# A broadcast row of per-token scales, made by two transfers through DRAM in place of a diagonal and a product with ones on TensorE

## The chip, the cores and the metric

The kernel runs on one core of a Trainium2 chip. The metric is the time of one execution on the device in microseconds (us), as the median of several runs. Beside it stands one profiled execution, whose trace gives the start and the length of every instruction on the engines: TensorE (PE, with its weight loads as PEld), VectorE (DVE), ScalarE (ACT), GpSimd (POOL) and SyncE (SP). DMAs are issued from the queues of SP and of POOL.

## The reference

Three residual blocks are applied to one sequence of 256 tokens with 2048 channels, all in float32: an attention layer that keeps the best keys by an index score, a block attention layer, and a third block of three-way sparse attention beside a gated linear recurrence, which ends in a gated feed-forward network (FFN). Each one begins with a root-mean-square norm:

```
def rms_norm(x, g):
    xf = x.astype(jnp.float32)
    y = xf * lax.rsqrt(jnp.mean(xf * xf, axis=-1, keepdims=True) + EPS)
    return (y * g.astype(jnp.float32)).astype(x.dtype)
...
    h2 = rms_norm_2(x, norm2_w[l])
    x = x + (jax.nn.silu(h2 @ w_ffn_gate[l]) * (h2 @ w_ffn_up[l])) @ w_ffn_down[l]
```

The norm's factor is one number for each token. The kernel multiplies by the gain before a product with the weights and by the token's factor after it, so that the product need not wait for the factor.

## The kernel before, in words

Tokens stand in two tiles of 128 partitions. The products with the weights stream about 394 MB, nearly all of it float32 weights, in tiles `raw` of mostly 1 MB from DRAM (queue of SP, three buffers). `weights` splits each half of a tile into a rounded part `wh` (ACT, line 135) and a rest `wl` (DVE, line 136), three buffers each, and PE multiplies both with the split activations. There are two kinds of product. `gemm` leaves tokens on the partitions; there the factor is a column of 128 numbers, one on each partition, which an engine takes as a scalar operand. `gemm_T` leaves channels on the partitions and tokens along the row; there the factor has to be a row of 256 numbers that stands on all 128 partitions. `row_of` makes that row from the two columns, and `joined` (lines 209 to 213) multiplies an evacuated product by it: two passes of `add_halves` (ACT line 206, DVE line 207) free the PSUM bank, then one DVE instruction multiplies by the row (line 213).

`row_of` is called five times: once in each of the two attention layers (`attn_layer`, line 595, the row is used from the gate products on), twice in `second` (line 1215), and once at the start of `ffn` (line 1373), where the first gate product is the next one to be evacuated. The columns come from `norm_rstd`: for each token tile a DVE sum (line 310) and four short POOL instructions (lines 298, 299, 313, 314).

Beside that work POOL issues small loads: the gains of the norms in set-up (`gains`, line 393), the constants of the third block (`gains2`, lines 405 to 408), the weights of its compression (`compress`, line 1036, read by the products `hid` in line 1044), the copy of x to DRAM (`park_x`, line 381), and the last gain in `ffn` (line 1376). Each engine works through its own list in order. The lists are laid out by the program's scheduler, which orders instructions by when it thinks they can run, with small side jobs deferred to steps of the large products; buffers come from rotating pools (`w2` has 28 buffers of 128x512). So an edit in one place can move instructions in another.

Of the kernel before, what the change touches and what calls it, by code (L numbers as in the profile page):

```python
# [11 lines left out]
F32 = mybir.dt.float32  # L12
F32R = mybir.dt.float32r
AF = mybir.ActivationFunctionType
ALU = mybir.AluOpType
AX = mybir.AxisListType

P = 128
T = 256
# [7 lines left out]
class Kern:  # L27
# [187 lines left out]
    def row_of(self, r):  # L215

        nc = self.nc
        b = self.bank("row")
        row = self.sb.tile([P, T], F32, tag="row", bufs=2, name="row")
        dg = self.w2("diag")[:, :T]  # L220
        for t in range(2):
            ts = slice(t * P, (t + 1) * P)
            nc.vector.tensor_scalar(dg[:, ts], self.ident, r[t], None, ALU.mult)
            nc.tensor.matmul(b[:, ts], self.ones, dg[:, ts], start=True, stop=True)
        nc.scalar.copy(row, b[:, :T])
        return row[:, None, :].to_broadcast([P, 2, T])

    def gemm_by_tile(self, xT, W, c0, n, evac, ng):
# [122 lines left out]
    def setup(self):  # L351
        nc, d, sb = self.nc, self.d, self.sb
        self.x = [[self.w2(f"x{t}{j}") for j in range(4)] for t in range(2)]
        self.load_x(0, d["x"][0])
        self.ident = sb.tile([P, P], F32, name="ident")
        nc.sync.dma_start(self.ident, d["c_ident"])
        zero = self.w2("zero")
        nc.vector.memset(zero, 0.0)
        warm = self.bank("warm")
        for _ in range(2):  # L360
            nc.tensor.matmul(warm, zero[:, :P], zero, start=True, stop=True)
        self.mhalf = sb.tile([P, 8], F32, name="mhalf")
        nc.vector.memset(self.mhalf, -0.5)
        self.ones = sb.tile([P, P], F32, name="ones")
        nc.vector.memset(self.ones, 1.0)
        self.gT = sb.tile([P, 64], F32, name="gT")
        g1 = self.w2("g1")[:, :P]
        nc.sync.dma_start(g1[:16, :], d["a_norm"].rearrange("a (k p) -> (a k) p", p=P))
        b = self.bank("gt")
        nc.tensor.transpose(b[:, 0:16], g1[:16, :], self.ident[:16, :16])  # L370
        nc.vector.tensor_copy(self.gT[:, 0:16], b[:, 0:16])
# [1194 lines left out]
```

## Time and profile before

| | |
|---|---|
| median of 3 runs | 2296.4 us (2295.2 to 2296.54) |
| the profiled execution's own time | 2295.19 us |
| its span in the trace | 2293.4 us, so 1.8 us lie around it |
| busy: PE, DVE, ACT, POOL | 99%, 65%, 50%, 6% of the span |
| mean granted clock of TensorE | 0.998 of full speed |
| weights and other data read from DRAM | 397.95 MB, 175 GB/s over the span |

The busy shares are means over the whole span. A line of the chain of waits or of the timeline says at which moment which engine was late; only there is an instruction worth its own length.

### The profile page before, as it was taken

To read this page: it belongs to the slowest core of one execution; us is meant where nothing else is said; L and a number is where in the kernel's file an instruction comes from. 1 tells how busy PE (TensorE), PEld (TensorE's weight loads), DVE (VectorE), ACT (ScalarE), POOL (GpSimd) and SP (SyncE) were. 2 spreads that over 40 slices of the span, in tenths; PEclk is the share of its full clock that TensorE was granted. 3 is DMA by queue.
4 is the path that set the end of the run, shared out by engine and by line. 5 is a ranking of instruction groups with operands and counts; after the bars stand their busy time and mean duration, and the time that the engine had idled before them with its cause. 6 is when DMAs were issued, how large, how long until landed. Compare 5 with 4: busy or idle time off the path is not lost.

```text
span 2293.4 us, 33719 instructions
## 1 busy us (share of the span) xinstructions
PE 2276.4 (99%) x13374; PEld 1939.6 (85%) x13374; DVE 1480.4 (65%) x2297; ACT 1146.2 (50%) x1966; POOL 136.0 (6%) x233
## 2 busy tenths in 40 slices
PE   9999999999999999999999999999999999999998
PEld 8878888888888888888888988888888888888887
DVE  5686775656775556789586666656665466655655
ACT  5555654556654434565563545545443344434444
POOL 1011100112100200000110000000000000000000
PEclk9999999999999999999999999999999999999999
DMA  7544455654456844454453576556555555555554
GB/s 228 189 159 147 129 184 183 190 184 147 152 184 202 250 141 149 132 161 151 134 173 111 177 227 192 185 183 202 184 184 190 194 185 184 186 195 188 184 186 145
DMA packets 308094, 404.33 MB, mean 176 GB/s; under 512 B 7376, under 2 KB 222384, under 8 KB 307936
## 3 DMA queue, kind: packets, MB, share of 16 engines
q1 hardware_dynamic: 305184, 394.04, 53.7%
q0 software_dynamic: 2752, 8.13, 1.2%
q8 instruction: 105, 1.72, 0.3%
q14 instruction: 53, 0.43, 0.1%
HBM read 397.95 MB, written 4.19 MB: 175 GB/s over the span
## 4 chain that ended last, share of the span: by engine, by line
PE 98%; DVE 1%; ACT 0%; DMA 0%; issue 0%; SPq 0%; POOL 0%; ACTq 0%; POOLq 0%
PE mm L189 31%; PE mm L191 16%; PE mm L163 14%; PE mm L164 14%; PE mm L165 14%; PE lg L490 1%; PE tr L344 1%; PE tp L269 1%; PE hid L1044 1%; PE pt L523 0%; PE ib L688 0%; PE nl L1136 0%; DMA x<-in_x_dram 0%; DVE wl L136 0%; PE ov L540 0%; PE cvb L791 0%
## 5 line engine op out<-in xcount | busy, mean ns | idle before, releaser
L136 DVE TENSOR_TENSOR wl<-raw,wh 128x1024 fp32r<-128x1024 f32 (+4 forms) x760 | 902.7, 1188 | 664.7 <-ACT wh L135 655.8
L135 ACT CAST wh<-raw 128x1024 fp32r<-128x1024 f32 (+4 forms) x760 | 776.5, 1022 | 838.9 <-PE mm L165 457.3
L189 PE MATMUL mm<-hl,wh 128*128 128x512 f32 x3072 | 1076.4, 395 | 2.0 <-DVE raw L207 1.2
L191 PE MATMUL mm<-hl,wl 128*128 128x256 f32 x3072 | 850.1, 284 | 0.1
L189 PEld LDWEIGHTS mm<-hl,wh 128*128 128x128 f32 x3072 | 568.9, 188 | 122.6 <-DVE raw L207 1.4
L191 PEld LDWEIGHTS mm<-hl,wl 128*128 128x128 f32 x3072 | 576.9, 188 | 12.6 <-DVE wl L136 0.4
L164 PE MATMUL mm<-wl,hl 128*128 128x512 f32 (+4 forms) x1504 | 574.4, 383 | 0.2 <-DVE wl L136 0.2
L165 PE MATMUL mm<-wh,hl 128*128 128x512 f32 (+4 forms) x1504 | 570.0, 381 | 0.0
L163 PE MATMUL mm<-wh,hl 128*128 128x512 f32 (+4 forms) x1504 | 529.6, 382 | 0.0
L164 PEld LDWEIGHTS mm<-wl,hl 128*128 128x128 f32 x1504 | 283.5, 189 | 55.2 <-issue 0.6
L165 PEld LDWEIGHTS mm<-wh,hl 128*128 128x128 f32 x1504 | 283.1, 188 | 55.1 <-issue 1.5
L163 PEld LDWEIGHTS mm<-wh,hl 128*128 128x128 f32 x1504 | 281.4, 189 | 56.5 <-issue 1.3
L298 POOL TENSOR_SCALAR rsqv<-nsum 128x1 f32<-128x1 f32 x10 | 3.5, 350 | 1188.1 <-DVE nsum L1418 733.2
L283 ACT ACTIVATE hl<-tp,gT 128x256 fp32r<-128x256 f32 x64 | 27.6, 471 | 22.1 <-PE tp L269 20.0
L284 DVE SCALAR_TENSOR_TENSOR hl<-tp,gT,hl 128x256 fp32r<-128x256 f32 x64 | 28.5, 478 | 12.7 <-ACT hl L283 12.5
L504 ACT ACTIVATE lg<-lg,nb 128x128 f32<-128x128 f32 (+1 forms) x64 | 28.4, 445 | 14.8 <-POOL nb L497 14.8
L206 ACT COPY up<-mm 128x256 f32<-128x256 f32 x44 | 16.4, 373 | 32.3 <-PE mm L191 32.3
L206 ACT COPY sg<-mm 128x256 f32<-128x256 f32 x44 | 16.4, 372 | 32.1 <-PE mm L191 32.1
L780 DVE SCALAR_TENSOR_TENSOR cv<-raw,cols,cv 128x255 f32<-128x255 f32 (+2 forms) x72 | 31.9, 475 | 0.2
L207 DVE TENSOR_TENSOR sg<-mm,sg 128x256 f32<-128x256 f32 x44 | 18.5, 421 | 15.5 <-ACT sg L206 15.5
L302 ACT ACTIVATE junk<-x 128x512 bf16<-128x512 f32 (+1 forms) x42 | 25.6, 610 | 5.5 <-DMA x<-in_x_dram 2.1
L207 DVE TENSOR_TENSOR up<-mm,up 128x256 f32<-128x256 f32 x44 | 18.5, 421 | 13.5 <-ACT up L206 13.5
(389 smaller groups left out, 1534.9 us busy)
## 6 DMA issues: line engine op xcount, KB each, us to landing
raw<-in_w_in_dram SPq DMA_DIRECT2D x76, 1024.0 KB, 5.2
raw<-in_w_ffn_gate_dram SPq DMA_DIRECT2D x44, 1024.0 KB, 5.1
raw<-in_w_ffn_up_dram SPq DMA_DIRECT2D x44, 1024.0 KB, 5.2
raw<-in_w_ffn_down_dram SPq DMA_DIRECT2D x41, 1024.0 KB, 5.0
raw<-in_a_w_in_dram SPq DMA_DIRECT2D x40, 1024.0 KB, 5.2
raw<-in_b_w_in_dram SPq DMA_DIRECT2D x40, 1024.0 KB, 5.1
raw<-in_a_w_out_dram SPq DMA_DIRECT2D x16, 1024.0 KB, 5.1
raw<-in_b_w_out_dram SPq DMA_DIRECT2D x16, 1024.0 KB, 5.2
```

Of the source, the lines that this page charges most:

```text
L135: nc.scalar.copy(wh, raw[:, k * h:k * h + k])
L136: nc.vector.tensor_tensor(wl, raw[:, k * h:k * h + k], wh.bitcast(F32), ALU.subtract)
L163: nc.tensor.matmul(o, xh, wh[:, c], start=first, stop=False)
L164: nc.tensor.matmul(o, xh, wl[:, c], start=False, stop=False)
L165: nc.tensor.matmul(o, xl, wh[:, c], start=False, stop=last)
L189: nc.tensor.matmul(self.c2(pt[m]), wh[:, c, ms], hl[:, c], start=first, stop=False)
L191: nc.tensor.matmul(pt[m][:, :T], wl[:, c, ms], hl[:, c, 0], start=False, stop=last)
L206: self.nc.scalar.copy(o, bank[:, T:])
L207: self.nc.vector.tensor_tensor(o, bank[:, :T], o, ALU.add)
L284: nc.vector.scalar_tensor_tensor(lo[:, k], tp[:, c], g, hi[:, k].bitcast(F32), ALU.mult, ALU.subtract)
L504: nc.scalar.activation(lgs[u][:, i * S:(i + 1) * S], lgs[u][:, i * S:(i + 1) * S], AF.Exp, bias=nbs[u][:, i:i + 1], accum_out=sms[t][:, h0 ...
L780: v.scalar_tensor_tensor(o[:, s:], x[:, :T - s], self.convw[:, k:k + 1], o[:, s:], ALU.mult, ALU.add)
```

## The change

The row is no longer computed on PE. Each of the two columns (128 partitions, one number each) is written to a DRAM tile `line` of 256 numbers by a DMA of POOL's queue, and a third DMA of the same queue reads the 256 numbers back onto all 128 partitions. The diagonal tiles on DVE, the products with ones on PE, the copy out of PSUM on ACT, the PSUM bank and the tile of ones go away.

```diff
     def row_of(self, r):
 
         nc = self.nc
-        b = self.bank("row")
+        line = self.dr.tile([T, 1], F32, tag="line", bufs=2, name="line")
         row = self.sb.tile([P, T], F32, tag="row", bufs=2, name="row")
-        dg = self.w2("diag")[:, :T]
         for t in range(2):
-            ts = slice(t * P, (t + 1) * P)
-            nc.vector.tensor_scalar(dg[:, ts], self.ident, r[t], None, ALU.mult)
-            nc.tensor.matmul(b[:, ts], self.ones, dg[:, ts], start=True, stop=True)
-        nc.scalar.copy(row, b[:, :T])
+            nc.gpsimd.dma_start(line[t * P:(t + 1) * P, :], r[t])
+        nc.gpsimd.dma_start(row, line.rearrange("t o -> o t").to_broadcast([P, T]))
         return row[:, None, :].to_broadcast([P, 2, T])
...
-        self.ones = sb.tile([P, P], F32, name="ones")
-        nc.vector.memset(self.ones, 1.0)
```

The scheduler lays the lists out anew. At the start of `ffn` POOL's list before has the chain of the first token tile, then the four loads of the last gain (`gf`), then the chain of the second tile:

```order
L298 TENSOR_SCALAR rsqv<-nsum 128x1 [waits DVE_49]
L299 TENSOR_TENSOR rstd_14704<-rsqv,mhalf 128x1 [waits Pool_49]
L313 TENSOR_SCALAR rstd_14706<-rstd_14704 128x1 [waits Pool_49]
L314 TENSOR_SCALAR rstd_14708<-rstd_14704 128x1
L1376 DMA gf_14732<-in_norm_f_w_dram 128x512 [waits DMASW5_49,PE_49]
L1376 DMA gf_14733<-in_norm_f_w_dram 128x512 [waits DMASW6_49,DMASW3_49,PE_49]
L1376 DMA gf_14734<-in_norm_f_w_dram 128x512 [waits DMASW7_49]
L1376 DMA gf_14735<-in_norm_f_w_dram 128x512
L298 TENSOR_SCALAR rsqv<-nsum 128x1 [waits DVE_49]
L299 TENSOR_TENSOR rstd_14705<-rsqv,mhalf 128x1 [waits Pool_49]
L313 TENSOR_SCALAR rstd_14707<-rstd_14705 128x1 [waits Pool_49]
L314 TENSOR_SCALAR rstd_14709<-rstd_14705 128x1
```

In the changed kernel (whose line numbers are 3 lower from line 226 of before on, and 5 lower from line 366 on) the same place of POOL's list reads as follows; line 221 writes a column to DRAM and line 222 reads the row back:

```order
L1371 DMA gf_14718<-in_norm_f_w_dram 128x512 [waits DMASW4_49]
L295 TENSOR_SCALAR rsqv<-nsum 128x1 [waits DVE_49]
L296 TENSOR_TENSOR rstd_14690<-rsqv,mhalf 128x1 [waits Pool_49]
L310 TENSOR_SCALAR rstd_14692<-rstd_14690 128x1 [waits Pool_49]
L311 TENSOR_SCALAR rstd_14694<-rstd_14690 128x1
L221 DMA line<-rstd_14690 128x1 [waits DMASW5_49]
L295 TENSOR_SCALAR rsqv<-nsum 128x1 [waits DVE_49]
L296 TENSOR_TENSOR rstd_14691<-rsqv,mhalf 128x1 [waits Pool_49]
L310 TENSOR_SCALAR rstd_14693<-rstd_14691 128x1 [waits Pool_49]
L311 TENSOR_SCALAR rstd_14695<-rstd_14691 128x1
L221 DMA line<-rstd_14691 128x1 [waits DMASW6_49]
L222 DMA row<-line 128x256 [waits DMASW7_49,DMASW6_49,DMASW5_49]
```

The four gain loads now stand ahead of both chains. The read of the row waits for both writes (DMASW5 and DMASW6 are their completion semaphores), and POOL has nothing to issue behind it before the end of the program.

DVE's list at the first gate evacuation of `ffn` before, where `sg` is the tile that takes the product and line 213 the multiplication by the row:

```order
L136 TENSOR_TENSOR wl<-raw,wh 128x1024 [waits DVE_49,DMAHW5_49,PE_49,Activation_49]
L207 TENSOR_TENSOR sg_14742<-mm,sg_14742 128x256 [waits Activation_49]
L136 TENSOR_TENSOR wl<-raw,wh 128x1024 [waits PE_49,Activation_49]
L207 TENSOR_TENSOR sg_14742<-mm,sg_14742 128x256 [waits Activation_49]
L136 TENSOR_TENSOR wl<-raw,wh 128x1024 [waits DMAHW6_49,PE_49,Activation_49]
L213 TENSOR_TENSOR sg_14742<-sg_14742,row 128x512 [waits DVE_49]
L136 TENSOR_TENSOR wl<-raw,wh 128x1024 [waits PE_49,Activation_49]
```

And in the changed kernel:

```order
L207 TENSOR_TENSOR sg_14725<-mm,sg_14725 128x256 [waits Activation_49]
L136 TENSOR_TENSOR wl<-raw,wh 128x1024 [waits DVE_49,DMAHW5_49,PE_49,Activation_49]
L207 TENSOR_TENSOR sg_14725<-mm,sg_14725 128x256 [waits Activation_49]
L213 TENSOR_TENSOR sg_14725<-sg_14725,row 128x512 [waits DMASW7_49,DVE_49]
L136 TENSOR_TENSOR wl<-raw,wh 128x1024 [waits PE_49,Activation_49]
L136 TENSOR_TENSOR wl<-raw,wh 128x1024 [waits DMAHW6_49,PE_49,Activation_49]
```

The multiplication has moved ahead of one `wl`, and it now waits for the DMA that brings the row (DMASW7).

In `second`, the changed list of POOL puts the two reads of rows ahead of the loads of the compression weights, which before came straight behind the chain of the second token tile:

```order
L221 DMA line<-rstd_6828 128x1 [waits DMASW3_49]
L221 DMA line<-rstd_6830 128x1 [waits DMASW4_49,Pool_49]
L222 DMA row<-line 128x256 [waits DMASW5_49,DMASW3_49,DMASW1_49]
L222 DMA row<-line 128x256 [waits DMASW6_49,DMASW4_49,DMASW2_49]
L1031 DMA w_7153<-in_cmp_w_k_dram 128x4x128 [waits DMASW7_49,PE_49,Activation_49]
```

There the loads of `gains2`, which stood between the two chains, have moved far ahead.

## Rows read from the trace of the kernel before

**Rows 1.** The page, part 1: busy time, share of span, instructions.

```profile
PE 2276.4 (99%) x13374; PEld 1939.6 (85%) x13374; DVE 1480.4 (65%) x2297; ACT 1146.2 (50%) x1966; POOL 136.0 (6%) x233
```

**Rows 2.** Waits of PE: waiting line, releaser; us in total, times, longest.

```profile
PE tp L269 <- DMA x<-in_x_dram: 2.7, 2, 2.5
...
PE ov L539 <- ACT half L527: 1.3, 1, 1.3
PE mm L189 <- DVE raw L207: 1.2, 1, 1.2
PE mm L189 <- DVE gt L207: 0.8, 1, 0.8
```

**Rows 3.** Seven windows over the row products (sum); timeline of PE behind one.

```profile
sum 1.99, PE 1.99; mean PE 0.28
...
51.87 0.58 PE L163 MATMUL mm<-wh,hl 128*128 128x368 f32 x2
52.28 0.33 PE L164 MATMUL mm<-wl,hl 128*128 128x368 f32 x1
52.45 0.33 PE L165 MATMUL mm<-wh,hl 128*128 128x368 f32 x1
```

**Rows 4.** Users of the tile row: ns min/median/max, first and last start in us.

```profile
L213 DVE TENSOR_TENSOR sg<-sg,row x22: 687/692/693, 1564.5 to 2198.0; 128x512 f32<-128x512 f32 x22
...
L213 DVE TENSOR_TENSOR gt<-gt,row x16: 668/692/694, 263.3 to 680.2; 128x512 f32<-128x512 f32 x16
L213 DVE TENSOR_TENSOR raw<-raw,row x12: 620/682/693, 945.8 to 1111.0; 128x512 f32<-128x512 f32 x12
```

**Rows 5.** Timeline of POOL at the start of `ffn`: start us, length us.

```profile
1546.67 0.19 POOL L298 TENSOR_SCALAR rsqv<-nsum 128x1 f32<-128x1 f32 x1 [269.61 <-DVE nsum L310]
...
1547.89 0.26 POOL L314 TENSOR_SCALAR rstd<-rstd 128x1 f32<-128x1 f32 x1
1548.09 2.24 POOL L1376 DMA_DIRECT2D gf<-in_norm_f_w_dram  x4
1550.41 0.18 POOL L298 TENSOR_SCALAR rsqv<-nsum 128x1 f32<-128x1 f32 x1
...
1552.08 0.26 POOL L314 TENSOR_SCALAR rstd<-rstd 128x1 f32<-128x1 f32 x1
```

**Rows 6.** Transfers of tiles parked, gf and w; then packets of SP's queue.

```profile
DMA to landing us min/median/max: 5.5/6.7/8.0
DMA to landing us min/median/max: 4.0/6.3/7.5
DMA to landing us min/median/max: 3.3/8.0/11.8
q1 hardware_dynamic: 305184, 394.04, 53.7%
```

**Rows 7.** Timelines of DVE and of PE at the first gate evacuation.

```profile
1562.97 0.42 DVE L207 TENSOR_TENSOR sg<-mm,sg 128x256 f32<-128x256 f32 x1
1563.32 1.23 DVE L136 TENSOR_TENSOR wl<-raw,wh 128x1024 fp32r<-128x1024 f32 x1
1564.46 0.69 DVE L213 TENSOR_TENSOR sg<-sg,row 128x512 f32<-128x512 f32 x1
...
1567.76 0.63 PE L189 MATMUL mm<-hl,wh 128*128 128x512 f32 x2
1568.22 0.40 PE L191 MATMUL mm<-hl,wl 128*128 128x256 f32 x2
```

**Rows 8.** Timeline of POOL in `second`; chain of waits at the first `hid`.

```profile
777.81 0.86 POOL L1036 DMA_DIRECT2D w<-in_cmp_w_k_dram  x1
...
809.18 0.99 PE hid L1044 x8
```

**Rows 9.** Lines 393 and 397 in set-up: ns, first and last start us.

```profile
L393 POOL DMA_DIRECT2D g<-in_b_norm_dram x1: 589/589/589, 23.4 to 23.4; - x1
...
L397 PE MATMUL gt<-ident,g x1: 258/258/258, 39.5 to 39.5; 48*128 48x48 f32 x1
```

## Prediction

> **What bounds the kernel now.** I read the page first: PE is busy for 2276.4 of 2293.4 us, the other engines for 65% and less [rows 1]. A busy share can hide a slow stretch, so I looked next at what PE waits for. The whole list is short: 2.7 us for the first tiles of x, which nothing in this change touches, three waits in mid-kernel of 1.3, 1.2 and 0.8 us, and crumbs [rows 2]. The chain of waits is on PE for 98% of the span. So the kernel is as long as PE's list of instructions. An edit gives what it takes off that list, and costs what it makes PE wait.
>
> **What is removed from PE.** Ten products of 128x128 in float32 leave, which the trace records as twenty passes. Laying a window over each of the seven places where they stand gives 1.99 us in sum [rows 3]. A switch between these passes and the split products costs a little more: behind the row product of set-up two passes start within 52.28 - 51.87 = 0.41 us, where one alone takes 52.45 - 52.28 = 0.17 us [rows 3]. That is 0.07 us over, and it arises at the three places where the neighbours are products with weights; elsewhere the neighbours are transposes, which stay and need the switch anyway. The sum on PE is 1.99 + 3 x 0.07 = **2.2 us**.
>
> **What is removed elsewhere.** Ten diagonals on DVE, the tile of ones and five copies on ACT leave. Both engines have a third or more of the span free, and PE waited only 3.3 us in mid-kernel for anything, none of it on a row [rows 1, 2]. I count them as nothing: PE's long list hides them.
>
> **What is added, where it has time.** Fifteen DMAs come onto POOL's queue, ten of half a kilobyte and five of 128 KB, all together far under one percent of what SP moves. An issue takes POOL 2.24 / 4 = 0.56 us [rows 5]. The rows of the attention layers and of `second` have long cover: the column in set-up is ready before the loads that start at 23.4 us [rows 9], and the row's first use is at 263.3 us; the rows of `second` are made near 778 us and first used at 945.8 us [rows 4, 8]. What needs a look is who stands behind the waiting read on POOL's list. In set-up these are three gain loads, issued from 23.4 us on, whose transpose PE runs at 39.5 us [rows 9]. Now the first write adds 0.56 us ahead of the second chain, so the second write is issued near 24.0; with the longest landing of 8.0 us [rows 6] the read goes out at 32.0, the last of the three loads at 32.0 + 3 x 0.56 = 33.7, and with 7.5 us it lands at 41.2, 1.7 us late. With the middle values, 6.7 and 6.3 us, it lands at 24.0 + 6.7 + 1.7 + 6.3 = 38.7, in time. I take nothing, with up to 1.7 us at the far end. In `second` the compression loads stand behind two reads. Before, the first was issued at 777.81 and used at 809.18 us [rows 8]. Four issues of writes have taken the place of four loads that moved ahead, so the second write goes out at about the old time; 8.0 us of landing and two issues put the first load 9.1 us later, at 786.9, and even the longest landing of such loads, 11.8 us [rows 6], ends at 798.7. That is covered by ten microseconds.
>
> **What is added, where time is short: the start of the FFN.** Here the row is used by the next evacuation. POOL's chain of the first token tile lasts from 1546.67 to 1547.89 + 0.26 = 1548.15 us; that of the second lasts 1552.08 + 0.26 - 1550.41 = 1.93 us [rows 5]. In the new list the four gain loads stand ahead, and one write's issue between the chains: 1548.15 + 0.56 + 1.93 = 1550.64 us for the second write. No transfer like it is in the trace; the nearest are those between x and its parked copy in DRAM, half of which write to DRAM (5.5 to 8.0, middle 6.7 us), and for the read-back the broadcast gain loads at this very place, of twice the size (4.0 to 7.5, middle 6.3 us) [rows 6]. A landing cannot be less than nothing, so there is no gain beyond hiding it. The row is there at 1550.64 + 6.7 + 6.3 = **1563.6 us**, between 1560.1 and 1566.1.
>
> When is it wanted? DVE's second pass of `add_halves` ends at 1562.97 + 0.42 = 1563.39 us [rows 7]; in the new list the multiplication comes right there, ahead of a `wl` that before ran from 1563.32 us on [rows 7]. Behind a waiting multiplication stand that `wl`, the next ones, and on ACT the activation of `sg`. The PSUM banks are free by then, as the two passes have read them. So PE suffers only through `wl`. With three buffers, that one is two groups of products ahead: it ends at 1564.55 us, and by the spacing of PE's groups its first reader is the pass at 1568.22 us [rows 7]. The row may then come at 1568.22 - 1.23 - 0.69 = 1566.3 us, and 0.45 us earlier since the two row products of this place, a fifth of the 2.2 us, no longer stand on PE's list ahead of it: **1565.85 us**. My value of 1563.6 makes DVE wait 0.2 to 0.7 us and PE not at all. The late end, 1566.1, costs PE 0.25 us.
>
> **The sum.** The profiled execution took 2295.19 us, its span 2293.4 and 1.8 around it. The span loses 2.2 us: 2291.2, and 2293.0 with what lies around it. That execution was 1.2 us below the median of 2296.4, so for the median I predict **2294.2 us**, 0.1% less. Runs of before lie 1.3 us apart, so about 0.2% (4.6 us) is what a measurement can tell from no change, and this is less than half of it.
>
> **The rivals.**
> - *The moved instructions also clear PE's mid-kernel waits.* The lists were laid out anew, and 1.3 + 1.2 + 0.8 = 3.3 us of waits are there to win [rows 2]. All of them gone gives 2296.4 - 2.2 - 3.3 = 2290.9 us, faster by 0.24%. Against it: these waits hang on attention steps whose neighbourhood in the lists reads the same in both kernels. 8%.
> - *The writes are slow because they are single numbers (slower).* Each write is 128 packets of four bytes. SP's packets take 0.537 x 16 x 2293.4 / 305184 = 0.065 us of an engine each [rows 6]; if all 128 of a write went one behind the other, that is 8.3 us on top. The row then comes at 1550.64 + 8.0 + 8.3 + 7.5 = 1574.4 us, 8.6 us after 1565.85, and the time is 2296.4 - 2.2 + 8.6 = 2302.8 us, slower by 0.28%. It decides from 6.8 us late on, which is write and read together at 22.0 us. Against it: no transfer that these rows show took over 11.8 us, and that one in a burst of large loads [rows 6]. 9%.
> - *POOL cannot issue while DVE works.* Suppose that each of the three issues at the FFN waited for two DVE instructions of 1.23 us [rows 7]: 7.4 us more, the row at 1571.0, 5.2 us late, 2299.4 us. That is still within 0.2%. The Trainium skill (SBUF — State Buffer, "SBUF: two separate sides") warns of this: DMAs from GpSimd's queue have descriptors written by GpSimd, which some DVE instructions lock out, and it measured 3100 ns for a DMA that takes 620 ns alone. By that page's figure three DMAs would be an estimated 7.4 us later, much as worked out here. The trace does not bear it out here: the four gain loads were issued in 2.24 us beside a busy DVE, at 0.56 us each [rows 5]. 5%.
> - *Nothing comes of it,* because other engines fill the 2.2 us: 2296.4 us. The chain on PE speaks against it. 8%.
>
> **How the numbers follow.** The forecast (PE shorter by 2.2 us, every row in time) has 69%. Faster by over 0.2% has the first rival, 8%; slower has the second, 9%, and 1% for mishaps of reordering that I can't name; the rest, 82%, is within 0.2%. The range goes down to the first rival and up past the third, with the 1.7 us of set-up allowed for in part: 2290.5 to 2300.0 us.
>
> **What would show it.** The trace after should have no row products on PE and about 2.2 us less span. The second write of the FFN should be issued near 1548.8 us (1550.64 less four fifths of 2.2 us, for the four rows ahead of it), and the row's multiplication begin within a microsecond of the second `add_halves`. In PE's list of waits no line with a `wl` at the FFN's start and no `gt` transpose in set-up should appear. The prediction is wrong if DVE's multiplication waits for the row by more than 2.5 us, if the `hid` products wait for their weights, or if an instruction far from the rows waits because a list was laid out otherwise.

## The result

The changed kernel takes **2312.8 us** in the median of 5 runs (2311.6 to 2313.2), the kernel before 2296.0 us (5 runs beside them). The ratio is 1.0073, with a 95% interval of 1.0062 to 1.0084: slower by 16.8 us, where 2294.2 was forecast. The span of the profiled execution went from 2293.4 to 2309.8 us. Where several executions were timed, a kernel's time is their median; one of the eleven behind experiment 10 took 10299 us and is left out of its ratio.

### The profile page after: what moved, and what is told of

Read it like the earlier page. It is cut to its first block, busy times and chain, and to the rows that moved or that the text cites. A ratio compares the mean times of both kernels' runs of the same rounds, so it can differ in the third digit from the quotient of the medians.

```text
span 2309.8 us, 33682 instructions
## 1 busy us (share of the span) xinstructions
PE 2279.0 (99%) x13354; PEld 1940.5 (84%) x13354; DVE 1477.7 (64%) x2286; ACT 1143.6 (50%) x1961; POOL 142.2 (6%) x248
## 4 chain that ended last, share of the span: by engine, by line
PE 95%; DMA 2%; DVE 1%; issue 1%; ACT 0%; POOL 0%; SPq 0%; ACTq 0%; POOLq 0%; DVEq 0%
PE mm L189 30%; PE mm L191 16%; PE mm L164 14%; PE mm L165 14%; PE mm L163 13%; PE lg L485 1%; PE tr L341 1%; DMA raw<-in_w_in_dram 1%; DMA line<-st 1%; PE tp L266 1%; PE hid L1039 1%; DVE wl L136 1%; PE pt L518 0%; DMA line<-rstd 0%; PE ib L683 0%
## 5 line engine op out<-in xcount | busy, mean ns | idle before, releaser
L281 DVE SCALAR_TENSOR_TENSOR hl<-tp,gT,hl 128x256 fp32r<-128x256 f32 x64 | 28.2, 478 | 12.9 <-ACT hl L280 12.7
L207 DVE TENSOR_TENSOR up<-mm,up 128x256 f32<-128x256 f32 x44 | 18.5, 421 | 13.6 <-ACT up L206 13.6
```

Source lines behind the costliest of these rows:

```text
L207: self.nc.vector.tensor_tensor(o, bank[:, :T], o, ALU.add)
L281: nc.vector.scalar_tensor_tensor(lo[:, k], tp[:, c], g, hi[:, k].bitcast(F32), ALU.mult, ALU.subtract)
```

## The profile after

First the busy line of the page, and then the list of what PE waits for, of the changed kernel; they answer to [rows 1, 2].

```profile
PE 2279.0 (99%) x13354; PEld 1940.5 (84%) x13354; DVE 1477.7 (64%) x2286; ACT 1143.6 (50%) x1961; POOL 142.2 (6%) x248
```

```profile
engine line waited for: us in total, times, longest us
PE mm L191 <- DVE wl L136: 6.6, 1, 6.6
PE gt L392 <- DMA g<-in_norm_w_dram: 4.3, 1, 4.3
PE tp L266 <- DMA x<-in_x_dram: 3.8, 1, 3.8
PE mm L163 <- ACT wh L135: 1.6, 1, 1.6
...
PE ov L534 <- ACT half L522: 1.3, 1, 1.3
PE mm L189 <- DVE raw L207: 1.2, 1, 1.2
PE mm L189 <- DVE gt L207: 0.8, 1, 0.8
```

The twenty passes of the row products are gone from PE (13374 before, 13354 now), and the three mid-kernel waits are the old ones. Three waits are new: 6.6 us for `wl` at the start of the FFN, 4.3 us for the gain loads and 1.6 us for `wh` in set-up. The busy line misleads: PE is busy for 2.6 us longer though it has less to do.

The clock explains that: PE works for 12.9 us at half its clock, where it was 3.4 before. These windows of the changed kernel cover the two stalls and what follows; the columns are the window with its length, then busy us and instructions of PE, PEld, DVE, ACT and POOL, the granted clock as a share of 2.4 GHz, the DMA share and GB/s.

```profile
43.90:46.90 3.00, 0.00 (x0) 0.02 (x1) 0.00 (x0) 0.81 (x1) 0.00 (x0) 0.50 0.93 293
46.90:50.70 3.80, 3.79 (x13) 3.71 (x14) 1.04 (x2) 0.08 (x1) 0.00 (x0) 0.51 0.15 54
50.70:54.40 3.70, 3.70 (x24) 3.70 (x24) 1.74 (x2) 1.54 (x2) 0.00 (x0) 1.00 0.24 45
1576.40:1579.70 3.30, 0.00 (x0) 0.00 (x0) 1.83 (x2) 1.10 (x2) 0.00 (x0) 0.50 0.10 20
1579.70:1583.20 3.50, 3.45 (x11) 2.97 (x12) 2.36 (x2) 1.41 (x2) 0.00 (x0) 0.50 0.64 207
1583.20:1587.00 3.80, 3.80 (x23) 3.35 (x22) 2.19 (x4) 1.71 (x4) 0.00 (x0) 1.00 1.06 351
```

PE stands still, its clock falls to 1.2 GHz, and after the stall it works on at that level for 3.8 and 3.5 us: 13 passes in the first of these, where the next 3.7 us hold 24. Half of that time, 1.9 and 1.8 us, is lost on top of the waits. The rest of the 12.9 us lies in the first loads of x.

**Where the 16.8 us are.** The start of the same PE instruction in both traces, after less before, gives the loss by place; it is called the shift below. It is 1.2 us by the end of the first loads of x, ahead of anything the change touches (it differs from -0.4 to 1.4 us between the kernels below). In set-up it grows to 9.0: 7.9 us, of which 4.3 + 1.6 + 1.9 = 7.8 account. By the middle it is 8.1, since row products have left. At the FFN it grows from 8.2 to 16.3 us: 6.6 + 1.8 = 8.4, less the two row products of this place.

**What is late.** POOL's timeline of the changed kernel at the FFN's start; it answers to [rows 5].

```profile
start us, us, engine line op out<-in xcount [idle before <-releaser]
1556.22 0.61 POOL L221 DMA_DIRECT2D line<-rstd  x1
...
1558.64 0.62 POOL L221 DMA_DIRECT2D line<-rstd  x1
1574.57 0.55 POOL L222 DMA_DIRECT2D row<-line  x1 [15.31 <-issue]
```

The read of the line waits 15.3 us behind the second write. DVE's timeline at the same place, which answers to [rows 7]:

```profile
1566.66 0.42 DVE L207 TENSOR_TENSOR sg<-mm,sg 128x256 f32<-128x256 f32 x1
1577.87 0.69 DVE L213 TENSOR_TENSOR sg<-sg,row 128x512 f32<-128x512 f32 x1 [10.79 <-DMA row<-line]
1578.48 1.22 DVE L136 TENSOR_TENSOR wl<-raw,wh 128x1024 fp32r<-128x1024 f32 x1
```

The multiplication waits 10.8 us for the row, and the `wl` that PE wants stands right behind it. In set-up the second write, issued at 24.69 us, lets the read go only at 40.41, and with it the gain loads:

```profile
24.69 0.62 POOL L221 DMA_DIRECT2D line<-st  x1
40.41 0.55 POOL L222 DMA_DIRECT2D row<-line  x1 [15.09 <-DMA line<-st]
40.95 0.52 POOL L388 DMA_DIRECT2D g<-in_b_norm_dram  x1
```

So a write of half a kilobyte lands after some 8 us if it is the first of two (11.4 and 11.9 us in `second`, where the first writes of two rows go out together) and after 15 to 17 us if it is the second. The second is itself held up: by the trace's records of packets, the packets of the FFN's first write start 1.2 to 1.4 us after its issue, those of the second 9.3 to 10.3 us after. The read-back is not slow: the chain of waits of the changed kernel has 3.20 us for it at the FFN.

**What else happens while a write is under way.** The window 437 to 456 us has the two writes of the second attention layer; first the kernel before, then the changed one (columns as above).

```profile
437.00:456.00 19.00, 19.00 (x83) 15.29 (x82) 11.76 (x15) 9.46 (x23) 6.06 (x6) 1.00 0.57 186
```

```profile
437.00:456.00 19.00, 19.00 (x87) 15.38 (x86) 9.70 (x11) 8.61 (x15) 2.35 (x7) 1.00 0.84 122
```

The DMA engines count as busy for 84% instead of 57% of the time and move a third less. In the trace's records of packets, 79 packets of SP's weight loads took over 2.5 us and up to 7.2 us, all where the writes are; a packet of 1024 bytes takes 0.046 us in the median, and before none of SP's took over 1.43 us. The writes' own packets, sixteen of 32 bytes for each write, are recorded with some 0.015 us. So it is the traffic behind a write that stands still. At this place PE does not feel it: its shift stays between 8.1 and 8.6 us.

## The experiments

Theory A at the start: each write is slow because it consists of four-byte numbers, and it costs where somebody waits for what comes behind it, the row at the FFN and the gains in set-up. The rivals: the held weight stream starves PE by itself (B); a trip through DRAM on POOL's queue is that slow in whatever form (C); an order of instructions that was laid out otherwise. The diffs show the main lines of each edit (... stands for the others) against the changed kernel, and in experiments 2, 6 and 10 against experiments 1, 4 and 5.

**1. The FFN's row by PE, the other four by DRAM.**

```diff
-    def row_of(self, r):
+    def row_of(self, r, place="mid"):
+        if place != "ffn":
             line = self.dr.tile([T, 1], F32, tag="line", bufs=2, name="line")
...
+        else:
+            b = self.bank("row")
+            dg = self.w2("diag")[:, :T]
...
+            nc.scalar.copy(row, b[:, :T])
```

> The FFN's row by PE as before, the other four rows by DRAM. Theory A (each slow write of 4-byte numbers costs where somebody waits for it: in set-up through the gain loads behind the read, at the FFN through the row): the FFN's part of the loss, 8.1 us by the shift of the markers, goes, the set-up's part stays; 2304.1 us, range 2303 to 2306, wait of gt for g still near 4.3 us, no wait of PE for wl near 1572 us. Rival (one loss spread over the kernel, such as an order of instructions laid out otherwise): the time is not split by place and stays above 2308 us.

Measured: 2310.8 us, ratio 1.0065 [1.0053, 1.0078]. The FFN's loss is gone (the shift stays at 15.6 us from the middle to the end), and set-up loses 9.8 us with a wait of 4.2 us for the gains. But `second` loses 5.1 us, where the shift of the changed kernel did not grow: PE waits up to 3.8 us for `wh` near 803 us, behind the writes there. That wait is for weights, which theory A had left out.

**2. Only the FFN's row by DRAM.**

```diff
-        if place != "ffn":
+        if place == "ffn":
```

> Only the FFN's row by DRAM, the other four by PE. Theory A: 2304.1 us, range 2303 to 2306, no wait of gt for g in set-up, and a PE wait for wl of 6 to 7 us at the FFN's start; this kernel's and the other one's losses add up to that of the whole change, 16.8 us. Rival (order laid out otherwise): they don't add up.

Measured: 2307.3 us, ratio 1.0047 [1.0034, 1.0059]. Nothing is lost up to the FFN, there 12.1 us; PE's wait for `wl` is 9.4 us. The place is confirmed, the size is not: the two losses make 14.7 + 11.2 = 25.9 us, not 16.8. What a write costs differs from kernel to kernel, even at one place.

**3. All rows by PE and used, with the writes and a short read beside them.**

```diff
+        b = self.bank("row")
+        dg = self.w2("diag")[:, :T]
...
+        nc.scalar.copy(row, b[:, :T])
         line = self.dr.tile([T, 1], F32, tag="line", bufs=2, name="line")
...
-        nc.gpsimd.dma_start(row, line.rearrange("t o -> o t").to_broadcast([P, T]))
+        nc.gpsimd.dma_start(row2, line[:64].rearrange("t o -> o t").to_broadcast([P, 64]))
```

> All five rows are made by PE and used, and the writes to DRAM and a read-back of 64 numbers are made too, with nobody using what is read. Theory A (late rows): at the FFN nothing is lost, as no one waits there; in set-up the gain loads still stand behind the read, so 8.6 us and the 0.5 us of row products that are back: 2305 us, range 2303.5 to 2307. Rival B (the writes hold up the weight stream, and that is what PE feels): the loss at the FFN stays as well, 2312 to 2315 us.

Measured: 2313.7 us, ratio 1.0081 [1.0067, 1.0095]. Theory A is refuted as the whole story: at the FFN PE waits 7.1 us for `wh`, behind a weight load for which ACT waits 9.0 us. (This is read from an execution of 2319.2 us, 5.6 us above the median.) It isn't a clean test, since the read came to stand ahead of POOL's second chain there and made it 5.8 us late.

**4. The line as one run.** PE transposes the columns into one partition.

```diff
-        line = self.dr.tile([T, 1], F32, tag="line", bufs=2, name="line")
+        line = self.dr.tile([1, T], F32, tag="line", bufs=2, name="line")
...
+        for t in range(2):
+            nc.tensor.transpose(b[0:1, t * P:(t + 1) * P], r[t], self.ident)
+        run = self.w2("run")[0:1, :T]
+        nc.scalar.copy(run, b[0:1, :T])
-            nc.gpsimd.dma_start(line[t * P:(t + 1) * P, :], r[t])
+        nc.gpsimd.dma_start(line, run)
...
```

> PE transposes the two columns into one partition (ten short transposes), the line goes to DRAM as one run of 1 KB, and is read back as in the change. Theory A (the 4-byte numbers make the write slow): the write lands in 2 to 5 us, the row is in time, no wait of gt or wl; 2295 us, range 2293 to 2297.5. Rival C (a trip through DRAM on this queue is that slow in whatever form): the waits stay, and the time is 2310 us or more.

Measured: 2295.2 us, ratio 0.9994 [0.9985, 1.0003]. No packet of SP took over 2.5 us, and no new wait appears. Rival C is refuted: queue and trip are the same, only the pieces differ.

**5. The writes alone.** The rows by PE, nothing is read back.

```diff
+        b = self.bank("row")
+        dg = self.w2("diag")[:, :T]
...
+        nc.scalar.copy(row, b[:, :T])
         line = self.dr.tile([T, 1], F32, tag="line", bufs=2, name="line")
         for t in range(2):
             nc.gpsimd.dma_start(line[t * P:(t + 1) * P, :], r[t])
-        nc.gpsimd.dma_start(row, line.rearrange("t o -> o t").to_broadcast([P, T]))
```

> All five rows by PE as before; the ten writes of 128 four-byte numbers are made too, nothing is read back and nobody waits for a write to land. Theory A (what is late is the row, and in set-up the gain loads behind the read): no stall is left but the 1.6 us for weights in set-up; 2296 to 2300 us. Rival B (each write holds the engines that move the weights, and that alone starves PE): PE waits for wh or wl by 4 us or more at one or more of the places of the writes; 2304 us or more.

Measured: 2314.0 us, ratio 1.0079 [1.0065, 1.0092], with all the loss of the change though nothing reads what is written. (The one wait for a write is that of the last write of `second`, 6.2 us for the one whose place in DRAM it takes over; the loads that PE waits for there were issued before it.) PE's waits in this kernel:

```profile
PE mm L189 <- ACT wh L135: 3.3, 1, 3.3
PE mm L163 <- ACT wh L135: 3.2, 2, 2.7
PE gt L413 <- DMA g<-in_conv_w_dram: 1.9, 1, 1.9
...
PE gt L414 <- DMA g<-in_dn_norm_w_dram: 1.7, 1, 1.7
```

Weights and small loads are late at set-up, `second` and the FFN; by the shifts, 7.1, 5.2 and 6.0 us are lost at the three, half clock included. Rival B holds: the writes alone are enough. In set-up the gains were issued from 25.4 to 26.4 us here, with no read ahead of them, and landed 16.0 to 16.7 us later (2.6 to 3.4 us in the kernel before); PE lost nearly as much. In the second attention layer the same writes cost PE nothing: the shift is 8.4 us ahead of them and 8.3 behind.

**6. A late row without slow writes.** The line of experiment 4 is copied four times in DRAM ahead of the FFN's read.

```diff
+        for k in range(hops):
+            far, line = line, self.dr.tile([1, T], F32, tag="hop", bufs=2, name="hop")
+            nc.gpsimd.dma_start(line, far)
         nc.gpsimd.dma_start(row, line.to_broadcast([P, T]))
```

> The lines go to DRAM as one run of 1 KB, which holds up nothing; in the FFN alone the line is then copied four times from DRAM to DRAM before it is read back, so that the row comes some 10 us later. Theory A: DVE's multiplication waits for the row, wl stands behind it, PE waits for wl at the FFN's start, by the row's lateness over 1566 us, and runs at 1.2 GHz for some us after it; with a row at 1576 some 10 us of wait and 2307 us in all. Rival B: without the hold of the weight stream a late row costs under 3 us, 2295 to 2298 us.

Measured: 2294.7 us, ratio 0.9996 [0.9987, 1.0005]. DVE's timeline shows why this doesn't decide:

```profile
1570.28 0.42 DVE L207 TENSOR_TENSOR sg<-mm,sg 128x256 f32<-128x256 f32 x1
1571.91 1.23 DVE L136 TENSOR_TENSOR wl<-raw,wh 128x1024 fp32r<-128x1024 f32 x1 [1.21 <-ACT wh L135]
1574.71 1.23 DVE L136 TENSOR_TENSOR wl<-raw,wh 128x1024 fp32r<-128x1024 f32 x1 [1.58 <-ACT wh L135]
1577.52 1.22 DVE L136 TENSOR_TENSOR wl<-raw,wh 128x1024 fp32r<-128x1024 f32 x1 [1.58 <-ACT wh L135]
1578.67 1.28 DVE L213 TENSOR_TENSOR sg<-sg,row 128x512 f32<-128x512 f32 x2
```

The scheduler knew of the copies and put the multiplication behind later `wl`. A multiplication at 1578.7 us, later than the 1577.9 of the changed kernel, which by then ran some 8 us behind, costs nothing. So lateness costs nothing here, where the list was laid out for a late row.

**7. The gains of set-up on SP's queue.**

```diff
-            nc.gpsimd.dma_start(g1[16 * i:16 * i + 16, :], ...
+            nc.sync.dma_start(g1[16 * i:16 * i + 16, :], ...
```

> The change, with the three gain loads of set-up issued on SP's queue, ahead of the read. Theory A: the wait of gt for g (4.3 us) and the half clock behind it (3.4 us) go; 2305 us, range 2303.5 to 2307. Rival B: the weights are held by the writes at the same time, PE waits for wh in place of g by 3 us or more; 2309 us or more.

Measured: 2318.5 us, ratio 1.0099 [1.0085, 1.0112], worse than the change. The gains were issued from 33.0 to 34.6 us, ahead of the read at 41.6, and landed 11.4 to 12.5 us later; PE waited 6.7 us for them. The read ahead of the gains is not what makes them late: while the writes are worked off, SP's transfers are late too.

**8. Probes of other shapes.** Rows as in experiment 4; each probe is one write (the last a read) in the FFN.

```diff
+                    if b == 0:
+                        self.probe(jb, u)
```

> Rows by one run of 1 KB; in eleven blocks of the FFN one probe each that nobody waits for: writes from 128 partitions of 4, 8, 16, 32 and 64 bytes each, of 4 bytes each 512 bytes apart, of 256 and of 512 bytes each, of 4 bytes from 32 partitions, of 4 bytes from 128 partitions issued by SP, and last a read of 4 bytes into each of 128 partitions. If the number of small pieces sets the price: all writes below 512 bytes land after 8 us or more beside packets of SP that take 2.5 us and more; the 512-byte write lands within 5 us and holds nothing; 32 partitions take a quarter of the hold, under 3 us; SP's queue is as slow as POOL's; 512 bytes apart is as slow. If neighbours in one stretch of DRAM are the cause: the write 512 bytes apart is quick. If POOL's queue is the cause: the write by SP is quick, and all others are slow, 512 bytes too.

**9. More probes,** with the distance and the count of four-byte numbers varied. The first probes had left theory D (only four-byte numbers at adjoining addresses hold the DMA engines) and rival E (any small numbers that share one small block of DRAM do).

> Rows by one run of 1 KB, eleven probes in the FFN that nobody waits for: 128 numbers of 4 bytes adjoining, then 8, 16, 32, 64 and 128 bytes apart, 16 and 64 numbers adjoining, 128 adjoining again, 128 pieces of 8 bytes issued by SP, 128 pieces of 12 bytes adjoining. Theory D (adjoining 4-byte numbers are held): the first, the ninth and in proportion to their count the seventh and eighth come with packets over 2.5 us, the others not. Rival E (numbers that share one small block of DRAM are held): those 8, 16 and 32 bytes apart are slow as well, and those 64 and 128 bytes apart are quick.

Measured: 2294.1 and 2293.9 us in one execution each; at these places of the FFN no wait of PE appears, so a hold by itself need not cost time. Results of both, worked out from the traces, each number from one transfer: the time from issue to landing, and the longest packet of SP's queue that starts within 14 us of the issue.

```
128 pieces, issued by POOL      us to landing    longest SP packet, us
4 B adjoining (three probes)    10.7 10.5 10.2   5.8 5.3 5.3
64 of 4 B adjoining             9.1              3.8
32 of 4 B adjoining             9.5              3.2
16 of 4 B adjoining             4.9              0.7
4 B, 8 / 16 / 32 B apart        6.0 5.1 5.0      0.6 0.7 1.1
4 B, 64 / 128 / 512 B apart     5.1 4.9 5.0      0.7 0.5 0.7
8 / 12 / 16 B adjoining         5.8 5.4 5.0      0.6 1.9 1.0
32 / 64 B adjoining             4.9 5.2          0.9 0.6
256 / 512 B adjoining           5.1 5.2          0.7 1.1
4 B read from DRAM              4.8              0.8
4 B adjoining, issued by SP     8.9              9.2
8 B adjoining, issued by SP     3.8              0.9
```

Of these shapes only four-byte numbers at adjoining addresses, written to DRAM, hold the engines. (The 1.9 us of the 12-byte pieces is no sign of a hold: experiment 10 below has a packet of 2.0 us far from any such write.) Each write that POOL issues goes out as sixteen packets, and the hold needs more than one number to a packet: 16 numbers are free, 32 and 64 are not. Its longest packet grows with their count, and SP's queue has it too, so POOL's queue is not the cause. My expectation that all pieces below 512 bytes are slow fell, and so did rival E: numbers 8 to 32 bytes apart share a small block as well.

**10. The control for experiment 5.** The same writes, 512 bytes apart.

```diff
-        line = self.dr.tile([T, 1], F32, tag="line", bufs=2, name="line")
+        line = self.dr.tile([T, P], F32, tag="line", bufs=2, name="line")
-            nc.gpsimd.dma_start(line[t * P:(t + 1) * P, :], r[t])
+            nc.gpsimd.dma_start(line[t * P:(t + 1) * P, 0:1], r[t])
```

> The kernel with all rows by PE and ten writes that nobody waits for, as before, but the numbers of a write lie 512 bytes apart in DRAM. Theory D: the loss of 18 us goes whole, 2296 us, range 2294.5 to 2297.5. Rival (ten more transfers on POOL's list, or another order of instructions, cost the 18 us): 2310 us or more.

Measured: 2295.6 us, ratio 0.9998 [0.9989, 1.0007]. All 18 us are gone, with the same ten transfers of the same size on the same queue. In the traces of experiments 5 and 10 every engine carries out the same instructions in the same order, so no other order can be the cause. The summary line of its writes:

```profile
DMA to landing us min/median/max: 1.8/3.3/5.5
```

**11. The change, mended.** Both columns side by side, one write of 8-byte pieces.

```diff
-        line = self.dr.tile([T, 1], F32, tag="line", bufs=2, name="line")
+        line = self.dr.tile([P, 2], F32, tag="line", bufs=2, name="line")
...
+        pair = self.small(2, "pair")
         for t in range(2):
-            nc.gpsimd.dma_start(line[t * P:(t + 1) * P, :], r[t])
+            nc.gpsimd.tensor_scalar(pair[:, t:t + 1], r[t], 1.0, None, ALU.mult)
+        nc.gpsimd.dma_start(line, pair)
...
-        self.nc.vector.tensor_tensor(o, o, row, ALU.mult)
+        o = o.rearrange("q h (t p) -> q h t p", t=2)
+        self.nc.vector.tensor_tensor(o, o, row[:, None].to_broadcast([P, 2, 2, P]), ALU.mult)
```

> The change with both columns of a row put side by side by two small POOL instructions and written in one transfer of 128 pieces of 8 bytes; the row is read back in one run and taken with a stride by DVE. If only 4-byte numbers at adjoining addresses hold the engines (theory D): no packet over 2.5 us, the write lands in 5 to 6 us, no wait of gt or wl, and what the prediction had expected comes: 2294 us, range 2292.5 to 2295.5. Rival (any scattered write between these loads costs): 2300 us or more.

Measured: 2293.3 us, ratio 0.9989 [0.9980, 0.9998]: faster than both kernels, than the one before by 2.6 us. No packet of SP's took over 2.0 us. DVE's timeline at the FFN's start:

```profile
1556.55 0.42 DVE L207 TENSOR_TENSOR sg<-mm,sg 128x256 f32<-128x256 f32 x1
1560.19 0.69 DVE L214 TENSOR_TENSOR sg<-sg,row 128x512 f32<-128x512 f32 x1 [3.22 <-DMA row<-line]
1560.80 1.22 DVE L136 TENSOR_TENSOR wl<-raw,wh 128x1024 fp32r<-128x1024 f32 x1
```

DVE waits 3.2 us for the row and PE not at all.

## Why the prediction was wrong

**The step that failed** is the landing of a line's write: 6.7 us, at most 8.0, from the `parked` transfers [rows 6]. Measured are 8.2 us for the first of two and 15 to 17 us for the second, because these writes are of a kind that no row of before showed. I weighed that as the second rival at 9%, with 8.3 us more and a row at 1574.4; it came at 1577.8 us. That rival named the right cause and the right sign, but it let only the write itself be slow, as 128 packets in a row. The trace has sixteen packets to a write, of 0.015 us each, so the writes' own packets are not where the time goes.

**The time at which the row is wanted** was wrong too. It was taken from the old list, with DVE ready at 1563.39 us. In the new lists the first gate product is evacuated sooner: the second `add_halves` ends at 1566.66 + 0.42 = 1567.08 us, which is 1558.9 without the shift of 8.2 us. PE bore 4.2 us of waiting behind that, so the row was wanted by 1563.1 and not by 1565.85, and even the 1563.6 of the forecast would have been half a microsecond late. The row came at 1577.8 - 8.2 = 1569.6, 6.0 us later than forecast, and was wanted 2.8 us sooner. Less the 2.2 us that were to spare, that gives the 6.6 us that PE waited.

**The step behind it** was to price fifteen DMAs by their volume, "far under one percent of what SP moves". What they block has to be counted, not what they move. Behind the writes packets took up to 7.2 us, and the weights and gains were late as well as the row. Experiments 5 and 10 show that this alone is worth 18 us when no one reads the line. The set-up step, "1.7 us at the far end", failed by it too: 7.9 us. Experiments 5 and 7 show that the gains are late there even if no read stands ahead of them.

**Which of the two, row or weights, sets the FFN's stall in the change?** The row, as the trace has it: `wl` starts as soon as the multiplication is through. Over four kernels whose lists have the multiplication at this place, DVE's wait and PE's go together: 13.6 and 9.4 us (experiment 2), 12.7 and 8.5 (7), 10.8 and 6.6 (the change), 3.2 and 0 (11). PE's is DVE's less 4.2 us. With the row taken away the weights take its place, at 6.0 us (experiment 5). A late row by itself in that list was not run.

**What was right.** The removal: in experiment 11 the shift falls by 2.0 us from set-up to the end, where 2.2 was worked out, and its 2293.3 us are 0.9 from the forecast. (Half of the 2.0 falls in `second`, which has two of the five rows. Experiment 10, with the row products still on PE, falls by 1.0 us there as well, so a part may be the order of the lists.) The read-back (3.2 to 6.6 us, taken 4.0 to 7.5), the issue of 0.54 to 0.63 us (0.56), DVE's order at the FFN (not its time), and the cover of the second attention layer's row held. PE's slack was mis-sized on the safe side: 2.5 us worked out, 4.2 measured. That POOL cannot issue while DVE works is not borne out: none of the fifteen issues took over 0.64 us, and beside the same DVE list as in experiment 5 the writes of experiment 10 landed in 1.8 to 5.5 us.

The Trainium skill ("DMA: Bandwidth & Descriptors", "Specifications") says that below 512 bytes a DMA does read-modify-write. Alone that rule doesn't explain these times: in the probes pieces of 8 to 256 bytes landed in 4.9 to 5.8 us, pieces of 512 in 5.2. What makes adjoining four-byte numbers so slow, and why the same numbers 8 bytes apart are free, stays open: no run shows what goes on inside a DMA engine.

## What to carry to other kernels

Price a small DMA by the shape of its pieces and by what it holds up behind it on all queues, not by its bytes: a column of four-byte numbers written to adjoining places in DRAM cost 8 us at each of two places here, and putting two numbers side by side, in one write, took all of it away. The same writes cost nothing in the second attention layer, so look at each place by itself. If a new transfer has no like in the trace, the range has to hold the case that it blocks the stream that feeds the bound engine. And look at where a consumer stands on its list: a row for which DVE waited 10.8 us was dear in a list laid out for an early one, and a row later still was free where the scheduler knew of its way.

## What was not expected of the hardware

A write of 512 bytes held SP's packets on the DMA engines for up to 7.2 us in the changed kernel, and for up to 9.2 us when SP issued it; the same bytes 8 bytes apart, or in pieces of 8 bytes, held nothing (no packet over 0.9 us near those probes). The trace books the hold to the packets queued behind the write, not to the write's own (0.015 us), so a busy share that rises (57% to 84%) while the GB/s fall (186 to 122) is what to look for.
